# Writing the zeros of a block-inverse scratch during layer 0 instead of at the start of layer 1, in a two-layer S5 + HGRN2 | RWKV-7 decoder step

## The chip, the cores and the metric

One core of a Trainium2 chip runs the kernel. The metric is device time of one execution, in microseconds (us). The engines named below are PE (TensorE, matmuls), DVE (VectorE), ACT (ScalarE), POOL (GpSimd) and SP (SyncE), whose queue issues every DMA of this kernel.

## The reference

One inference step of a decoder trunk with two layers, model width 1024, in float32, for a prompt of 1024 tokens and 8 decode sequences of 4 tokens. Every product that matters is a dense float32 matrix product, or a recurrence over tokens:

```python
# layer 0 (even)
proj = xn @ w['even_w_in'][j]
u, z_a, q, f, i, z_b = jnp.split(proj, EVEN_SPLITS, axis=-1)
...                                  # S5 scan on u, HGRN2 on q, f, i
out = jnp.concatenate([out_a, out_b], axis=-1) @ w['even_w_out'][j]
h = h + out
# layer 1 (odd): token shift, then r, k, v, z and three low-rank products
xr, xw, xk, xv, xa, xg = (xn + xx * mix[m] for m in range(6))
r = xr @ wp[0]
...
s = (s * w_t[:, :, None, :]
     - jnp.einsum('bhvk,bhk->bhv', s, kk_t)[..., None] * (kk_t * a_t)[:, :, None, :]
     + v_t[..., None] * k_t[:, :, None, :])
```

The kernel computes the RWKV-7 recurrence in chunks. In each chunk the delta rule needs the inverse of a triangular matrix, which is taken in diagonal blocks of 32x32 and then combined; the 64x64 matrix that holds the diagonal blocks' inverses is zero beside them. These zeros are what the change is about.

## The kernel before

**Dense products.** Float32 is done as three fp32r matmuls: an operand is split into a high part (ACT copy, line 70) and the remainder (DVE subtract, line 72), so `xh,wh`, `xl,wh` and `xh,wl` appear as three matmuls. `dense2` (line 800; its matmuls are recorded at line 805) accumulates a whole product in a PSUM bank `dps`, of which there are two (line 798), and hands the bank to a function that empties it. Weights come as 256 KB loads into `ws`, and are split into `wh` and `wl`.

**DMAs.** `dma` (lines 51 and 52) issues everything on SP's queue, in program order as the scheduler leaves it. Staging tiles of tag "ev" (`evt`, line 1033, three buffers of 128x544) hold what goes from PSUM to DRAM.

**Layer 0** (`layer0`, line 1871). `proj_in` makes the input projection of one output tile after another and writes tiles to DRAM (`pr<-ev`); `s5_part` is the S5 branch, mostly on DVE; `hgrn_head` loads a head's tiles back (`hf<-pr`, `hq`, `hi`, `hz`) and begins with three activations on ACT (lines 567 to 569) and a scan on DVE. `run` (line 1860) takes turns between such generators by given rates, and thereby sets the order in which the program is written.

**Between the layers.** `proj_out` multiplies by `even_w_out` and adds the bank into the residual tile `res` on DVE (line 757), after `res<-xT` has loaded it; the sum is stored (`h<-res`).

**Layer 1.** `l1_constants` (line 889) loads and transposes the token-shift state (matmuls `t<-ident,ZB`), and then writes the zeros: a staging tile `sX` is cleared on POOL (line 902), and eight DMAs of 128x1024 (512 KB) write it to the four DRAM tiles `x_d` (`xd<-sX`, lines 903 to 905), 4.19 MB in all. `mixed` (line 929) makes the six mixed inputs `mm` on DVE, which are split into `xh`, `xl`. `rwkv_inverse` works out the diagonal blocks' inverses with 31 steps on DVE, in the same tile `sX` (cleared on POOL at line 1399), and writes only the blocks into `x_d`; later the chain of a batch loads whole matrices from there (`DT`). That chain also loads `ZR`, `BK` and `DA`.

**What sets the order.** The program is written by these generators, and a list scheduler with a timing model of its own then orders each engine's instructions. Each engine runs its stream in that order. An instruction that waits holds up all that follow it on its engine.

Of the kernel before, what the change touches and what calls it, by code (L numbers as in the profile page):

```python
# [36 lines left out]
class Builder:  # L37
# [837 lines left out]
    def l1_vectors(self):  # L875
# [8 lines left out]
        self.omix = K("omix", 6 * KT)  # L884
        self.nc.vector.tensor_scalar(out=self.omix, in0=self.mix, scalar1=-1.0, scalar2=1.0, op0=ALU.mult, op1=ALU.add)

    def l1_constants(self, kp):
        nc, V = self.nc, self.nc.vector
        K = lambda name, *sh: kp.tile([128, *sh], F32, name=name)
        sl = self.stage("ZB", 2, KT, 128)[:, 0]  # L890
        self.dma(sl[:8].rearrange("p k f -> p (k f)"), self.I["state_shift"][0])
        ps = self.PS(KT, NB)
        for k in range(KT):
            nc.tensor.transpose(ps[:, k], sl[:8, k], self.ident[:8, :8])
        self.evac(self.sh, ps, KT * NB)

        self.rs1 = K("rs1", 544)
        V.memset(self.rs1, 1.0)
        V.memset(self.rs1[:, 0:512].rearrange("p (n c) -> p n c", c=64)[:, :, 0:1], 0.0)
        V.memset(self.rs1[:, 512:544].rearrange("p (b t) -> p b t", t=NS)[:, :, 0:1], 0.0)  # L900
        zero = self.stage("sX", 32, 32)
        nc.gpsimd.memset(zero, 0.0)
        for d in self.x_d[0] + self.x_d[1]:
            for c in range(0, 8, 4):
                self.dma(d[:, c:c + 4].rearrange("r c p t -> r (c p t)"), zero[:].rearrange("r s t -> r (s t)"))

    def pair(self, n):
        self.pairs += 1
# [962 lines left out]
    def layer0(self, st):  # L1871
        tc = self.tc
        P = lambda name, st, **kw: st.enter_context(tc.tile_pool(name=name, bufs=1, reuse_waits="tile", **kw))
        self.pq = P("l0ps", st, space=PSUM)
        self.keep, hk, hp = P("l0k", st), P("hgk", st), P("hg", st)
        self.rbc = [self.keep.tile([128, 544], F32, name=f"rbc{i}") for i in range(2)]
        self.done, self.xn = set(), []
        order = [b + h for h in range(4) for b in (12, 8, 16, 20)] + list(range(4, 8))
        with ExitStack() as s5:
            kp = P("s5k", s5)  # L1880
            with ExitStack() as t:
                tp, xp = P("s5t", t), P("x0", t)
                self.sm = xp
                x1 = [self.normed(1, k, x) for k, x in enumerate(self.load_x(xp, 1, self.keep))]
                for m, _ in enumerate(self.proj_in(1, x1, range(4))):
                    if m == 1:
                        self.l1_vectors()
                    if m == 0:
                        x0 = self.load_x(xp, 0, self.keep)
                self.s5_params(kp, tp)  # L1890
                x0 = [self.normed(0, k, x) for k, x in enumerate(x0)]
                for _ in self.proj_in(0, x0, range(4)):
                    pass
            self.hgrn_constants(hk)
            sp = P("s5", s5)

            def dense():
                yield from self.proj_in(0, x0, order)
                x1 = self.reload_x(1)
                yield from self.proj_in(1, x1, order)  # L1900

            def s5s():
                for m in range(4):
                    for e in range(2):
                        yield from self.s5_part(sp, m, e)
                self.s5_finish(sp)

            def heads():
                for hf in range(2):
                    for h in range(4):  # L1910
                        while not all((k + h, hf) in self.done for k in (8, 12, 16, 20)):
                            yield
                        yield from self.hgrn_head(hp, hf, h)

            hgrn = heads()
            self.run((dense(), 1), (s5s(), self.rate0[0]), back=(hgrn, self.rate0[1]))
        ready = lambda hf: all(("o", hf, h) in self.done for h in range(4))
        self.heads, self.glus = ([], []), ([], [])
        with ExitStack() as t:
            gp = P("glu", t)  # L1920

            def rest():
                glu = self.glu(0, gp, gp)
                while not ready(0):
                    yield
                next(glu)
                self.heads_out(0, gp)
                yield from glu
                yield from self.proj_out(0)

            self.run((rest(), 1), (hgrn, self.rate0[2]))
# [82 lines left out]
```

## Time and profile before

| what | us |
|---|---|
| median of 3 runs | 1889.67 (1886.45, 1889.67, 1898.71) |
| the profiled execution | 1892.82 |
| its span on the engines | 1891.1 |
| PE busy | 1706.0 |
| DVE busy | 1297.9 |
| ACT busy | 977.1 |
| POOL busy | 140.7 |

The span runs from the first to the last instruction that the profile shows; 1.72 us of the profiled execution lie around it. A busy time is the sum over the instructions of an engine. The mean granted TensorE clock was 0.911 of full speed. The DMA engines moved 163 GB/s on the mean. Times within the trace are in us from the start of the span.

### The profile page before, as it was taken

The numbers are of one execution on the slowest core, as the hardware profiler recorded it, in microseconds if no ns is written. First come the engines' busy times: TensorE is split into PE (matmuls) and PEld (weight loads), VectorE is DVE, ScalarE is ACT, GpSimd is POOL, SyncE is SP. The second block draws the span as 40 slices with busy tenths as digits, with TensorE's granted clock in tenths as the row PEclk, the third lists the DMA queues.
The fourth block names the chain that finished last, engine by engine and source line by source line (L and its number), as shares of the span: only waits on it lengthen the run. The fifth ranks groups of instructions, "written<-read, shape, count | busy, mean of one in ns | idle before, by whom it ended". The sixth has DMA issues, their size and how long they took to land. (4 is left out here: it accounts for less than half of the span.)

```text
span 1891.1 us, 39586 instructions
## 1 busy us (share of the span) xinstructions
PE 1706.0 (90%) x15060; PEld 1419.1 (75%) x15060; DVE 1297.9 (69%) x3010; ACT 977.1 (52%) x1886; POOL 140.7 (7%) x257
## 2 busy tenths in 40 slices
PE   4999989999997698997399999998899999999867
PEld 3877868988876576775377778887798887788756
DVE  5797798875678624789598734868968566565554
ACT  5445555555645334643356766645555435434454
POOL 1210011000004200011021000000000000000000
PEclk9899999888999797998599889989898998999799
DMA  8555554444562556699758234589794666453453
GB/s 205 173 157 141 136 149 130 138 131 123 172 186 84 173 184 200 185 255 262 194 141 203 81 125 161 146 226 243 206 220 120 178 159 166 126 157 104 118 157 106
DMA packets 555010, 308.39 MB, mean 163 GB/s; under 512 B 284883, under 2 KB 489043, under 8 KB 554820
## 3 DMA queue, kind: packets, MB, share of 16 engines
q1 hardware_dynamic: 554820, 305.86, 59.1%
q8 instruction: 119, 1.95, 0.4%
q14 instruction: 71, 0.58, 0.1%
HBM read 199.76 MB, written 104.81 MB: 161 GB/s over the span
## 5 line engine op out<-in xcount | busy, mean ns | idle before, releaser
L805 PE MATMUL dps<-xh,wh 128*128 128x272 f32 (+3 forms) x1696 | 581.2, 349 | 55.3 <-ACT xh L70 22.3
L805 PE MATMUL dps<-xl,wh 128*128 128x272 f32 (+3 forms) x1696 | 582.6, 346 | 18.7 <-DVE xl L72 18.1
L805 PE MATMUL dps<-xh,wl 128*128 128x272 f32 (+3 forms) x1696 | 575.3, 342 | 4.8 <-DVE wl L72 4.7
L805 PEld LDWEIGHTS dps<-xh,wh 128*128 128x128 f32 x1696 | 330.9, 198 | 108.2 <-ACT xh L70 27.0
L805 PEld LDWEIGHTS dps<-xl,wh 128*128 128x128 f32 x1696 | 334.5, 198 | 60.9 <-DVE xl L72 28.1
L805 PEld LDWEIGHTS dps<-xh,wl 128*128 128x128 f32 x1696 | 335.0, 198 | 37.7 <-DVE wl L72 8.4
L70 ACT ACTIVATE wh<-ws 128x512 fp32r<-128x512 f32 (+1 forms) x336 | 195.9, 619 | 289.9 <-PE dps L805 198.8
L72 DVE TENSOR_TENSOR wl<-ws,wh 128x512 fp32r<-128x512 f32 (+1 forms) x336 | 224.1, 685 | 97.6 <-ACT wh L70 96.7
L1514 PE MATMUL m<-ZR,BK 64*128 64x128 f32 x512 | 62.8, 296 | 21.4 <-DMA ZR<-zr 20.6
L1514 PEld LDWEIGHTS m<-ZR,BK 64*128 64x128 f32 x512 | 54.0, 196 | 28.7 <-issue 14.3
L70 ACT ACTIVATE xh<-mm 128x256 fp32r<-128x256 f32 (+1 forms) x112 | 52.8, 481 | 37.5 <-DVE mm L929 19.7
L72 DVE TENSOR_TENSOR xl<-mm,xh 128x256 fp32r<-128x256 f32 (+1 forms) x112 | 55.6, 507 | 5.6 <-ACT xh L70 2.6
L805 PE MATMUL dps<-gh,wh 128*128 128x272 f32 (+1 forms) x176 | 55.8, 317 | 2.1 <-ACT ev L1106 1.1
L805 PE MATMUL dps<-gl,wh 128*128 128x272 f32 (+1 forms) x176 | 54.8, 312 | 1.4 <-DVE gl L72 1.4
L805 PE MATMUL dps<-gh,wl 128*128 128x272 f32 (+1 forms) x176 | 54.5, 310 | 0.1
L1411 DVE TENSOR_TENSOR sT<-sX,sN 128x31 f32<-128x31 f32 (+15 forms) x124 | 42.1, 339 | 11.9 <-DMA sN<-nd 10.2
L66 DVE COPY ev<-dps 128x272 f32<-128x272 f32 (+1 forms) x43 | 22.5, 526 | 40.2 <-PE dps L805 35.0
L64 ACT ACTIVATE ev<-dps 128x272 f32<-128x272 f32 (+1 forms) x65 | 29.3, 450 | 37.5 <-PE dps L805 37.1
L1571 PE MATMUL m<-ZM,DT 64*64 64x128 f32 x512 | 41.1, 291 | 2.4 <-DVE MR L1517 2.4
L1417 DVE TENSOR_TENSOR sX<-sX,sT 128x31 f32<-128x31 f32 (+15 forms) x124 | 42.0, 339 | 1.7
L863 POOL COPY edge<-h 128x1 f32<-128x1 f32 x8 | 27.1, 3392 | 182.6 <-DVE h L850 182.5
L805 PEld LDWEIGHTS dps<-gh,wh 128*128 128x128 f32 x176 | 35.1, 199 | 6.3 <-ACT ev L1106 1.6
(644 smaller groups left out, 3365.1 us busy)
## 6 DMA issues: line engine op xcount, KB each, us to landing
ws<-in_rw_w_rkvz SPq DMA_DIRECT2D x128, 256.0 KB, 4.2
ws<-in_even_w_in SPq DMA_DIRECT2D x96, 256.0 KB, 3.7
ws<-in_rw_w_o SPq DMA_DIRECT2D x48, 256.0 KB, 3.1
ws<-in_even_w_out SPq DMA_DIRECT2D x32, 256.0 KB, 3.8
BK<-bk SPq DMA_DIRECT2D x32, 256.0 KB, 4.4
ZR<-zr SPq DMA_DIRECT2D x32, 256.0 KB, 2.7
pr<-ev SPq DMA_DIRECT2D x20, 272.0 KB, 2.0
pr<-ev SPq DMA_DIRECT2D x20, 256.0 KB, 3.9
```

The lines of the kernel that those rows point to most:

```text
L64: return self.nc.scalar.activation(out, in_, AF.Copy)
L66: return self.nc.vector.tensor_copy(out, in_)
L70: self.nc.scalar.activation(hi, x, AF.Copy)
L72: e.tensor_tensor(out=lo, in0=x, in1=hi.bitcast(F32), op=ALU.subtract)
L805: mm = lambda c0, n, i, u, k, v: self.nc.tensor.matmul(ps[c0], u[:, k, :], v[:, c0:c0 + n], start=i == 0, stop=i == len(terms) - 1)
L863: G.tensor_copy(self.edge[:, k:k + 1], x[:, 512:513])
L1411: E.tensor_tensor(out=w, in0=X[:, s0:s0 + m, j:j + 1].broadcast_to([128, m, n]), in1=N[:, j, j + 1:32].unsqueeze(1).broadcast_to([128, m, ...
L1417: E.tensor_tensor(out=X[:, s0:s0 + m, j + 1:32], in0=X[:, s0:s0 + m, j + 1:32], in1=w, op=ALU.subtract)
L1514: nc.tensor.matmul(f2(pm[h][:, q]), f2(BK[hr, q]), f2(ZR[hr, q]), start=True, stop=True)
L1571: nc.tensor.matmul(pd[hr, q], DT[hr, q], ZM[hr, q], start=True, stop=True)
```

## The change

The zeros are written by a new generator, `clear_inverses`, which takes turns with the dense products and the S5 branch of layer 0 at a rate of 0.5. It clears 512 columns of one "ev" tile on POOL and issues 16 DMAs of 128x512 (256 KB), one at each turn. `l1_constants` loses the cleared tile and its eight DMAs. The bytes are the same.

```diff
--- before.py
+++ after.py
@@ -884,6 +884,15 @@
         self.omix = K("omix", 6 * KT)
         self.nc.vector.tensor_scalar(out=self.omix, in0=self.mix, scalar1=-1.0, scalar2=1.0, op0=ALU.mult, op1=ALU.add)
 
+    def clear_inverses(self):
+
+        zero = self.evt("zero")
+        self.nc.gpsimd.memset(zero[:, 0:512], 0.0)
+        for d in self.x_d[0] + self.x_d[1]:
+            for c in range(0, 8, 2):
+                self.dma(d[:, c:c + 2].rearrange("r c p t -> r (c p t)"), zero[:, 0:512])
+                yield
+
     def l1_constants(self, kp):
         nc, V = self.nc, self.nc.vector
         K = lambda name, *sh: kp.tile([128, *sh], F32, name=name)
@@ -898,11 +907,6 @@
         V.memset(self.rs1, 1.0)
         V.memset(self.rs1[:, 0:512].rearrange("p (n c) -> p n c", c=64)[:, :, 0:1], 0.0)
         V.memset(self.rs1[:, 512:544].rearrange("p (b t) -> p b t", t=NS)[:, :, 0:1], 0.0)
-        zero = self.stage("sX", 32, 32)
-        nc.gpsimd.memset(zero, 0.0)
-        for d in self.x_d[0] + self.x_d[1]:
-            for c in range(0, 8, 4):
-                self.dma(d[:, c:c + 4].rearrange("r c p t -> r (c p t)"), zero[:].rearrange("r s t -> r (s t)"))
 
     def pair(self, n):
         self.pairs += 1
@@ -1913,7 +1917,7 @@
                         yield from self.hgrn_head(hp, hf, h)
 
             hgrn = heads()
-            self.run((dense(), 1), (s5s(), self.rate0[0]), back=(hgrn, self.rate0[1]))
+            self.run((dense(), 1), (s5s(), self.rate0[0]), (self.clear_inverses(), 0.5), back=(hgrn, self.rate0[1]))
         ready = lambda hf: all(("o", hf, h) in self.done for h in range(4))
         self.heads, self.glus = ([], []), ([], [])
         with ExitStack() as t:
```

The scheduler's order changes with it. SP's queue in layer 0, where the dense products' weights (`ws`) are loaded and the first HGRN2 head's tiles (`pr_73` is its input `f`) are stored and loaded back; before, from the load of `ws` behind `u_88<-us`:

```order
L52 DMA ws<-in_even_w_in 128x4x128
L52 DMA pr_73<-ev 128x512
L52 DMA ws<-in_even_w_in 128x4x128
L52 DMA hf<-pr_73 128x512
L52 DMA pr_69<-ev 128x512
L52 DMA ws<-in_even_w_in 128x4x128 x2
L52 DMA hq<-pr_69 128x512
L52 DMA pr_77<-ev 128x512
L52 DMA ws<-in_even_w_in 128x4x128 x2
L52 DMA hi<-pr_77 128x512
```

and in the changed kernel, where the 16 writes `xd<-zero` stand from behind `u_88<-us` to ahead of `hq`:

```order
L52 DMA xd_121<-zero 128x512 x2
L52 DMA ws<-in_even_w_in 128x4x128
L52 DMA pr_73<-ev 128x512
L52 DMA ws<-in_even_w_in 128x4x128
L52 DMA xd_121<-zero 128x512 x2
L52 DMA xd_122<-zero 128x512 x2
L52 DMA hf<-pr_73 128x512
L52 DMA xd_122<-zero 128x512 x2
L52 DMA xd_123<-zero 128x512
L52 DMA pr_69<-ev 128x512
L52 DMA ws<-in_even_w_in 128x4x128
L52 DMA xd_123<-zero 128x512
```

Six of the 256 KB writes now stand ahead of `hf<-pr_73`, and the other ten between it and `hq`.

DVE in layer 0, where the first head's subtract (line 570) and scan (line 572) stand among the S5 branch's steps (lines 358 to 363) and the splits `wl`, as a piece of the difference:

```order
-L570 SCALAR_TENSOR_TENSOR hl<-hf,hl 128x512
 L361 TENSOR_SCALAR t_974<-t_974 128x256
 L359 TENSOR_TENSOR t_975<-ji 128x256
+L362 TENSOR_TENSOR jr<-jr,t_974 128x32x8
+L363 TENSOR_TENSOR ji<-ji,t_974 128x32x8
+L358 TENSOR_TENSOR t_974<-jr 128x256
+L72 TENSOR_TENSOR wl<-ws,wh 128x512
+L360 TENSOR_TENSOR t_974<-t_974,t_975 128x256
+L72 TENSOR_TENSOR wl<-ws,wh 128x512
+L361 TENSOR_SCALAR t_974<-t_974 128x256
+L570 SCALAR_TENSOR_TENSOR hl<-hf,hl 128x512
```

The two weight splits `wl` moved from behind the head's scan to ahead of the head's first DVE instruction.

DVE at the start of layer 1, where `res` is the first residual add of `proj_out` that follows the token-shift transposes, `mm` and `xl` are the mixed inputs and their low parts, and `blkm` and `hsel` are constants; before:

```order
L72 TENSOR_TENSOR wl<-ws,wh 128x512
L1219 CAST blkm<-e_6752 128x128
L72 TENSOR_TENSOR xl<-mm,xh 128x512 x2
L1254 COPY e_6800<-t 2x128 x4
L929 SCALAR_TENSOR_TENSOR mm<-df_6660,mix,h_6118 128x512
L929 SCALAR_TENSOR_TENSOR mm<-df_6666,mix,h_6157 128x512
L1255 CAST hsel<-e_6800 2x128 x4
L72 TENSOR_TENSOR xl<-mm,xh 128x512 x2
L929 SCALAR_TENSOR_TENSOR mm<-df_6672,mix,h_6196 128x512
L929 SCALAR_TENSOR_TENSOR mm<-df_6678,mix,h_6235 128x512
L72 TENSOR_TENSOR xl<-mm,xh 128x512 x2
L929 SCALAR_TENSOR_TENSOR mm<-df_6636,mix,h_5962 128x512
```

It goes on with one more `mm`, and then `L757 TENSOR_TENSOR res<-res,dps 128x272 x2`. In the changed kernel:

```order
L72 TENSOR_TENSOR wl<-ws,wh 128x512
L933 SCALAR_TENSOR_TENSOR mm<-df_6672,mix,h_6097 128x512
L72 TENSOR_TENSOR wl<-ws,wh 128x512
L757 TENSOR_TENSOR res<-res,dps 128x272 x2
L1223 CAST blkm<-e_6770 128x128
L72 TENSOR_TENSOR xl<-mm,xh 128x512 x2
L1258 COPY e_6818<-t 2x128 x4
L933 SCALAR_TENSOR_TENSOR mm<-df_6678,mix,h_6136 128x512
L933 SCALAR_TENSOR_TENSOR mm<-df_6684,mix,h_6175 128x512
L1259 CAST hsel<-e_6818 2x128 x4
L72 TENSOR_TENSOR xl<-mm,xh 128x512 x2
L933 SCALAR_TENSOR_TENSOR mm<-df_6690,mix,h_6214 128x512
```

The two adds `res` moved ahead of six splits `xl`, six mixed inputs `mm` and the constants, and the order of those is unchanged.

PE there, from the token-shift transposes `t<-ident,ZB` on, where the 512-column matmuls are the first product of layer 1 and those of 272 columns the next tile of `proj_out`; before:

```order
L894 MATMUL t<-ident,ZB 128x8 x8
L805 MATMUL dps<-xh,wh 128x512
L805 MATMUL dps<-xl,wh 128x512
L805 MATMUL dps<-xh,wl 128x512
L805 MATMUL dps<-xh,wh 128x512
L805 MATMUL dps<-xl,wh 128x512
L805 MATMUL dps<-xh,wl 128x512
L805 MATMUL dps<-xh,wh 128x512
L805 MATMUL dps<-xl,wh 128x512
L805 MATMUL dps<-xh,wl 128x512
L805 MATMUL dps<-xh,wh 128x512
```

It goes on with the rest of 24 matmuls of 512 columns, and then 48 of 272 columns. In the changed kernel:

```order
L903 MATMUL t<-ident,ZB 128x8 x8
L805 MATMUL dps<-xh,wh 128x512
L805 MATMUL dps<-xl,wh 128x512
L805 MATMUL dps<-xh,wl 128x512
L805 MATMUL dps<-xh,wh 128x512
L805 MATMUL dps<-xl,wh 128x512
L805 MATMUL dps<-xh,wl 128x512
L805 MATMUL dps<-xh,wh 128x512
L805 MATMUL dps<-gh,wh 128x272
L805 MATMUL dps<-gl,wh 128x272
L805 MATMUL dps<-gh,wl 128x272
```

The matmuls of 272 columns moved in between those of 512: behind the seven of 512 stand 14 of 272, then 5 of 512, 3 of 272, 1 of 512, 7 of 272, 11 of 512 and the last 24 of 272.

On SP's queue the load `res<-xT_57` stood behind the zeros (`ws<-in_rw_w_rkvz`, six `xd<-sX`, two `w2s`, two `xd<-sX`, `ws<-in_even_w_out`, `res<-xT_57`). In the changed kernel it stands right behind `ws<-in_rw_w_rkvz`.

## Rows read from the trace of the kernel before

**Rows 1.** The page: busy time, share of the span and instructions of each engine.

```profile
PE 1706.0 (90%) x15060; PEld 1419.1 (75%) x15060; DVE 1297.9 (69%) x3010; ACT 977.1 (52%) x1886; POOL 140.7 (7%) x257
```

**Rows 2.** Waits of PE: line, releaser, us in total, times, longest us.

```profile
PE m L1514 <- DMA ZR<-zr: 20.6, 2, 10.9
...
PE dps L805 <- DVE res L757: 17.5, 2, 15.3
```

**Rows 3.** PE's timeline, layer 1's start: start, us, then [idle before <-releaser].

```profile
627.87 0.66 PE L894 MATMUL t<-ident,ZB 8*128 8x8 f32 x8
643.87 0.77 PE L805 MATMUL dps<-xh,wh 128*128 128x512 f32 x1 [15.34 <-DVE res L757]
644.43 0.63 PE L805 MATMUL dps<-xl,wh 128*128 128x512 f32 x1
644.86 0.63 PE L805 MATMUL dps<-xh,wl 128*128 128x512 f32 x1
...
651.28 0.29 PE L805 MATMUL dps<-gh,wh 128*128 128x272 f32 x1
651.40 0.28 PE L805 MATMUL dps<-gl,wh 128*128 128x272 f32 x1
```

**Rows 4.** DVE's timeline there.

```profile
632.54 0.69 DVE L72 TENSOR_TENSOR wl<-ws,wh 128x512 fp32r<-128x512 f32 x1
...
640.69 1.35 DVE L72 TENSOR_TENSOR xl<-mm,xh 128x512 fp32r<-128x512 f32 x2
...
643.29 0.78 DVE L757 TENSOR_TENSOR res<-res,dps 128x272 f32<-128x272 f32 x2
```

**Rows 5.** SP's timeline there (its DMA issues).

```profile
625.75 0.43 SPq L52 DMA_DIRECT2D ws<-in_rw_w_rkvz  x1
626.28 5.65 SPq L52 DMA_DIRECT2D xd<-sX  x6
...
634.50 1.15 SPq L52 DMA_DIRECT2D xd<-sX  x2
...
636.50 1.28 SPq L52 DMA_DIRECT2D res<-xT  x1
```

**Rows 6.** Tile res, 600 to 720: time from issue to landing.

```profile
DMA to landing us min/median/max: 2.8/2.9/4.6
```

**Rows 7.** SP's timeline, layer 0.

```profile
108.52 0.52 SPq L52 DMA_DIRECT2D u<-us  x1
...
112.51 0.37 SPq L52 DMA_DIRECT2D ws<-in_even_w_in  x1
115.33 0.34 SPq L52 DMA_DIRECT2D hf<-pr  x1
```

**Rows 8.** ACT's timeline, layer 0.

```profile
118.19 0.64 ACT L567 ACTIVATE hl<-hf 128x512 f32<-128x512 f32 x1 [3.92 <-DMA hf<-pr]
...
122.71 1.13 ACT L70 ACTIVATE wh<-ws 128x512 fp32r<-128x512 f32 x2
```

**Rows 9.** Windows: PE, PEld, DVE, ACT, POOL busy (instructions), clock, DMA share, GB/s.

```profile
108.00:116.00 8.00, 8.00 (x36) 6.54 (x35) 8.00 (x52) 3.04 (x4) 0.00 (x0) 1.00 0.59 164
628.00:632.00 4.00, 0.53 (x8) 0.43 (x8) 3.82 (x13) 1.94 (x4) 0.00 (x0) 0.84 1.04 419
880.00:900.00 20.00, 9.81 (x81) 4.71 (x81) 17.67 (x42) 10.29 (x15) 6.45 (x12) 0.59 1.01 272
```

**Rows 10.** Tile ws, 108 to 130: time from issue to landing.

```profile
DMA to landing us min/median/max: 3.1/3.6/4.1
```

**Rows 11.** PE's timeline, layer 0.

```profile
124.38 0.50 PE L805 MATMUL dps<-xh,wh 128*128 128x512 f32 x1 [1.58 <-ACT ev L64]
...
127.19 0.80 PE L805 MATMUL dps<-xh,wl 128*128 128x512 f32 x1 [2.08 <-DVE wl L72]
```

**Rows 12.** PE's timeline, the chain of the first batches.

```profile
903.80 3.06 PE L1514 MATMUL m<-ZR,BK 64*128 64x128 f32 x16 [9.71 <-DMA ZR<-zr]
...
908.27 1.08 PE L1381 MATMUL t<-ZB 64*32 64x32 f32 x64
```

## The prediction

> **What bounds the kernel now.** I read the page's busy times first. PE is busy for 90% of the span, DVE for 69% [rows 1]. So over most of its length the kernel is a stream of matmuls, and a change of this kind can only win or lose in the places where PE stands still. The second view was the list of PE's waits. Two of its entries lie where this change works or just behind: 17.5 us for the residual add on DVE (line 757), of which 15.3 us in one piece, and 20.6 us for the load `ZR` [rows 2].
>
> The third view was PE's timeline around the long piece. PE ends the eight small transposes that begin at 627.87 and starts its next matmul at 643.87, after 15.34 us in which it waited for `res` on DVE [rows 3]. The two PSUM banks `dps` are full of an output-projection tile, and nothing else can go into them before DVE has added them into `res`. DVE's timeline tells why this comes late: the two adds stand in DVE's order behind a row of splits and mixed inputs. The split `wl` starts at 632.54, the last two `xl` end at 640.69 + 1.35 = 642.04, and the adds start at 643.29, with no idle time noted before any of these [rows 4]. In the same stretch SP issues the zeros, and `res<-xT` is issued at 636.50 behind them, where the weight load ahead of them went out at 625.75 [rows 5].
>
> **Layer 1's start, what is removed.** The eight writes of zeros go, and SP's 5.65 + 1.15 = 6.8 us of issuing them [rows 5]. The load of `res` then stands right behind the weight load, so it is issued at 625.75 + 0.43 = 626.2 and, with the usual 2.9 us and at most 4.6 us from issue to landing [rows 6], is there by 631. The adds stand behind the `wl` of 632.54, so they can start at 632.54 + 0.69 = 633.2 in place of 643.29, which is 10.1 us earlier. What is late next is PE's own work together with the `xl` splits. PE has 24 matmuls of 512 columns (643.87 to 651.28, 7.4 us with a slow start) and 48 of 272 columns, 0.12 us apart (5.8 us) [rows 3]. In the new order the two kinds alternate, so that PE can work on the second while DVE still makes the `xl` for the first. The last `xl` comes at 642.04 plus the 0.78 us of the adds, 642.8 [rows 4]. By then PE can have done the matmuls that don't need it, and the end of this piece moves from 651.28 + 5.8 = 657.1 to 633.8 + 13.2 = 647.0, a gain of 10.1 us. That is one bound. For the other I let the last 11 of the 512-column matmuls and 24 of the 272-column ones all wait for 642.8, at half the clock. Half the clock is the spacing of 644.43 and 644.86, 0.43 us, and twice 0.12 us for the short ones [rows 3]: 11 x 0.43 + 24 x 0.24 = 10.5 us, end 653.3, gain 3.8 us. I take 9.5, near the upper end, since the alternating order leaves PE enough to do before 642.8 (13 x 0.43 + 24 x 0.12 = 8.5 us of work for 9.0 us of time).
>
> **Layer 0, what is added.** 16 writes of 256 KB, 4.19 MB, go into SP's queue between `u<-us` at 108.52 and the load `hq`, six of them ahead of the load `hf`, which is issued at 115.33 [rows 7]. SP's issuing costs nothing by itself: SP has empty time between its issues there, such as 2.5 us ahead of 115.33, for 0.3 to 0.5 us an issue [rows 7]. What counts is the transfer. The window from 108 to 116 carries 164 GB/s. The highest rate that the trace shows, just when the zeros of before are written, is 419 GB/s; a stretch full of 256 KB loads reaches 272 GB/s, at a full DMA share too [rows 9]. In the 6.8 us from 108.52 to 115.33 the spare rate moves 1.73 MB at the one and 0.73 MB at the other, against six writes of 1.57 MB. So `hf` lands between 0 and (1.57 - 0.73) MB / 272 GB/s = 3.1 us late. ACT waits for it with nothing in hand (idle for 3.92 us until 118.19 [rows 8]), and its order is unchanged there, so the delay goes through ACT to the weight splits behind.
>
> For all 4.19 MB the same sum until 122.71 leaves 0.57 MB, or 1.4 us, at 419 GB/s, and 2.66 MB, or 9.8 us, at 272. A weight load has slack: issued at 112.51 [rows 7], landed after 3.6 us [rows 10], split at 122.71 [rows 8], 6.6 us spare. The excess is 0 to 3.2 us. With a restart of PE at half the clock (12 matmuls of 512 columns, 0.43 us [rows 3] in place of 0.12 x 512/272 = 0.23 us: 2.4 us) the worst is 3.1 + 3.2 + 2.4 = 8.7 us. Below nothing, the new order of DVE puts the `wl` splits ahead of the head's scan, and PE's two gaps there, 1.58 and 2.08 us [rows 11], may close: -3.7 us. I take +2, nearer to the 419 row because its transfers are the same writes, with two thirds of the 3.1 us for `hf`.
>
> The Trainium skill speaks against the smaller pieces. In "DMA: Bandwidth & Descriptors", section "Bandwidth", it asks for transfers of 1 MiB and gives 341 GB/s for 1 MB and 138 GB/s for 64 KB. [...]
>
> **The rest.** POOL clears one tile in either kernel, on an engine that is busy for 7% of the span [rows 1]: nothing. `zero` holds one of three "ev" tiles while the writes last; a store of `pr` that needs it would wait in the same stretch, which is inside the bound of 8.7 us. The scheduler's order moves almost everywhere by a few places. A single place that goes well or badly is worth about one of PE's larger waits, 9.7 us [rows 12], so I bound it by 10 us on either side and take nothing.
>
> **Sum.** 1892.82 - 9.5 + 2 = 1885.3 for an execution like the profiled one. That one lies 3.15 us above the median of 1889.67, so I predict 1882.2, rounded 1882. The bounds of the two priced terms give -13.8 to +4.9, or 1876 to 1895: this is the forecast's own range.
>
> **Rivals.**
> - *The gain is given back later, no change.* Around 880 to 900 the DMA engines are full (share 1.01) and PE is busy for less than half of the time [rows 9]; PE waits for `ZR` 20.6 us in all [rows 2]. If the loads there, and not PE, set the time, PE that comes 9.5 us earlier waits 9.5 us longer. What remains is the 2 us of layer 0: 1891.7. Against it: these loads and what fills them start earlier too when the stages ahead do, since the same queue issues everything.
> - *Slower: the zeros block layer 0.* `hf` is 3.1 us late, the last ten writes keep `hq` back by 9.8 us, ACT waits for both in its order, and PE runs out of split weights and restarts at half the clock (2.4 us): 15.3 us lost. The gap at layer 1's start gives 3.8. Then 1889.67 + 11.5 = 1901.2. It decides from the point where PE's lost time between 108 and 140 is over 9.5 us. For it: ACT's idle time before `hf`. Against: 6.6 us of slack in the weight loads, and a rate of 419 GB/s for such writes.
> The same skill page, section "Two DMAs through the same engine are not ordered", says that descriptors of one queue start in order on an engine; by that `hf` can't overtake the zeros. No row of before shows it.
> - *Faster by more: the first batches close a gap as well.* In the new order 32 of the small transposes `t<-ZB` (64 in the row at 908.27) stand ahead of the first `m<-ZR,BK`, where before they follow PE's wait of 9.71 us [rows 12]. If with them and the earlier start that wait closes: 1882.2 - 9.7 = 1872.5. Against it: 1.08 us of transposes fill little of it, and the load itself would have to come earlier.
>
> **Chances.** The forecast 0.59, no change 0.20, slower 0.09, faster by more 0.12. One per cent (18.9 us) is about what a measurement of this kernel can tell from no change: faster means 1870.8 or less, slower 1908.6 or more. The forecast's own range lies within 1%, and so does the rival without a change. The faster rival lies just inside, and I give half of it and a share of the unpriced order, 0.12, to faster; half of the slower one, 0.05, to slower. The range for 8 in 10 reaches from 1868, a little below the faster rival, to 1898, between the forecast's worst and the slower rival.
>
> **What would show it.** Right: PE's wait for `res` at layer 1's start shrinks from 15.34 to 5 or 6 us; the DMA share near 628 to 636 falls; `res<-xT` is issued near 626; in layer 0 `hf` lands by about 120 and PE's gaps between 120 and 130 stay within 6 us. The rest of the stages then keep their length and only start earlier. Wrong: the adds start late though `res` is there; PE's wait for `ZR` grows by what was won; `hq` or a split `wl` releases PE after a wait of several us near 120 to 140; or a wait of PE elsewhere, which this text does not name, grows or goes by 5 us or more.

## The result, and the profile of the changed kernel

The changed kernel takes 1907.74 us (median of 14 runs, 1901.03 to 1923.73), the kernel before 1896.8 us (14 runs on the same footing, 1886.19 to 1906.96). The ratio is 1.0071, 95% interval 1.005 to 1.0093: slower by 0.7%, outside the range of 1868 to 1898 us and on the other side of no change. The median of 1889.67 us that the forecast started from was that of three runs; the 14 lie 7 us higher, which explains part of the distance to 1882 but not the sign.

The profiled execution of the changed kernel took 1901.03 us, 8.2 us more than the one before. Its page, span and busy times first, as in [rows 1]:

```profile
span 1899.3 us, 39597 instructions
...
PE 1724.5 (91%) x15060; PEld 1433.6 (75%) x15060; DVE 1297.3 (68%) x3010; ACT 973.7 (51%) x1883; POOL 141.4 (7%) x257
```

PE's busy time grew from 1706.0 to 1724.5 us, by 18.5 us. Its idle time, span minus busy, fell from 1891.1 - 1706.0 = 185.1 to 1899.3 - 1724.5 = 174.8 us, by 10.3 us. So PE waited less, as was forecast, and yet took longer for the same 15060 matmuls: they ran at a lower clock. The granted clock of the profiled execution was 0.899, before 0.911. Each of these is one execution, and the clock also varies between executions of one order: x1 below, which has the order of the kernel before, has PE busy for 1731.8 us at 0.897 in its profile, more than the changed kernel:

```profile
PE 1731.8 (91%) x15060; PEld 1441.4 (75%) x15060; DVE 1298.8 (68%) x3010; ACT 977.6 (51%) x1886; POOL 145.7 (8%) x257
```

So the 18.5 us can't all be laid to the order. What can is shown further down: the times of all runs, their mean clock, and the stretches that agree over several profiles.

PE's waits in the changed kernel (line, releaser, us in total, times, longest), as in [rows 2]:

```profile
PE t L1385 <- DVE ZB L1340: 11.4, 2, 8.6
...
PE m L1518 <- DMA ZR<-zr: 8.1, 2, 7.6
PE m L1529 <- DVE Q L1596: 6.9, 2, 5.4
PE dps L805 <- DVE res L757: 6.1, 2, 5.4
```

The wait for `res` went from 17.5 to 6.1 us and the wait for `ZR` from 20.6 to 8.1 us. Two waits on DVE are new or grown: 11.4 us for `ZB`, and 6.9 us for `Q`, which was 0.6 us. Most of the first is no loss of its own. In the new order the transposes `t<-ZB` stand ahead of the first `m<-ZR,BK`, so PE waits 8.63 us for `ZB` where it waited 9.71 us for `ZR` [rows 12], and the wait for `DA` behind it is longer; the changed kernel, and then the kernel before:

```profile
894.75 1.08 PE L1385 MATMUL t<-ZB 64*32 64x32 f32 x64 [8.63 <-DVE ZB L1340]
...
914.56 0.70 PE L1552 MATMUL m<-DA,MZ 32*32 32x32 f32 x16 [11.43 <-DMA DA<-xnd]
```

```profile
919.61 0.81 PE L1548 MATMUL m<-DA,MZ 32*32 32x32 f32 x16 [8.62 <-DMA DA<-xnd]
```

Layer 1's start, the three rows that answer to [rows 3 to 5]: PE, DVE and SP of the changed kernel.

```profile
642.35 0.77 PE L805 MATMUL dps<-xh,wh 128*128 128x512 f32 x1 [5.36 <-DVE res L757]
```

```profile
641.77 0.78 DVE L757 TENSOR_TENSOR res<-res,dps 128x272 f32<-128x272 f32 x2
```

```profile
634.42 0.42 SPq L52 DMA_DIRECT2D ws<-in_rw_w_rkvz  x1
634.89 0.50 SPq L52 DMA_DIRECT2D res<-xT  x1
```

The load of `res` stands right behind the weight load (0.47 us, before 10.75 us behind it), the adds follow the second `wl`, and PE waits 5.36 us in place of 15.34. These are the steps as forecast.

Layer 0 of the changed kernel, SP and then ACT and PE, as in [rows 7, 8, 11]:

```profile
107.39 1.24 SPq L52 DMA_DIRECT2D xd<-zero  x2
...
111.28 2.61 SPq L52 DMA_DIRECT2D xd<-zero  x4
114.69 0.32 SPq L52 DMA_DIRECT2D hf<-pr  x1
115.06 1.46 SPq L52 DMA_DIRECT2D xd<-zero  x3
...
120.25 3.81 SPq L52 DMA_DIRECT2D xd<-zero  x6
```

```profile
119.07 0.63 ACT L567 ACTIVATE hl<-hf 128x512 f32<-128x512 f32 x1 [7.00 <-DMA hf<-pr]
```

```profile
125.26 0.80 PE L805 MATMUL dps<-xh,wh 128*128 128x512 f32 x1 [4.12 <-ACT ev L64]
```

`hf` is issued at 114.69 and starts ACT's activation at 119.07, 4.4 us later, where it took 2.9 us before. The 16 writes drive the DMA engines to their full share; the windows (PE, PEld, DVE, ACT, POOL busy, clock, DMA share, GB/s), as in [rows 9]:

```profile
108.00:116.00 8.00, 7.66 (x33) 5.63 (x32) 8.00 (x43) 3.04 (x4) 0.00 (x0) 1.00 1.02 312
116.00:124.00 8.00, 5.14 (x22) 3.86 (x21) 5.28 (x14) 4.87 (x7) 0.00 (x0) 0.95 1.05 358
```

PE's idle time there is one wait of 4.12 us, against 1.58 + 2.08 = 3.66 us before. In this execution PE waits 0.5 us more at this place.

Then one of the places where time went. In the stage of the batches PE works at half the clock while it is busy all the time. The windows of the changed kernel:

```profile
1030.00:1050.00 20.00, 18.62 (x259) 14.88 (x258) 16.52 (x42) 18.07 (x43) 0.00 (x0) 0.87 0.36 112
1050.00:1070.00 20.00, 20.00 (x125) 15.62 (x124) 14.78 (x40) 13.20 (x37) 0.00 (x0) 0.50 0.20 53
1070.00:1090.00 20.00, 20.00 (x127) 16.79 (x127) 6.37 (x15) 5.86 (x12) 0.00 (x0) 0.78 0.23 73
```

and of the kernel before, in which the same work runs about 8 us later:

```profile
1050.00:1070.00 20.00, 18.17 (x174) 14.06 (x174) 16.14 (x41) 15.72 (x39) 0.00 (x0) 0.66 0.24 69
1070.00:1090.00 20.00, 20.00 (x221) 17.58 (x216) 12.01 (x31) 10.96 (x27) 0.00 (x0) 1.00 0.28 85
```

From 1050 to 1090 PE of the changed kernel is busy for 40.00 of 40 us and gets through 252 matmuls; before, it gets through 395 in those 40 us, with 1.8 us idle (the two mixes of short and long ones are not the same). The trace's record of the granted clock has one stretch at half the clock of 34.1 us there (from 1044.8), where before it has one of 13.7 us (from 1054.0). No list of waits shows this, since nothing waits. The rows of PE around the fall:

```profile
1041.41 0.68 PE L1541 MATMUL m<-ident,ZR 64*64 64x64 f32 x16
1042.54 0.87 PE L1545 MATMUL m<-L,MZ 64*64 64x64 f32 x6 [0.45 <-ACT L L1576]
1043.91 0.39 PE L805 MATMUL dps<-xl,wh 128*128 128x272 f32 x1 [0.50 <-DVE xl L72]
...
1046.66 0.64 PE L1552 MATMUL m<-DA,MZ 32*32 32x32 f32 x16
```

and of the kernel before, where the clock falls at the same work:

```profile
1050.76 0.87 PE L1541 MATMUL m<-L,MZ 64*64 64x64 f32 x6 [0.93 <-DVE L L66]
...
1053.47 0.44 PE L1548 MATMUL m<-DA,MZ 32*32 32x32 f32 x16 [0.90 <-DVE ZM L66]
```

So the fall itself is in both kernels, with longer waits ahead of it in the old one. What differs is how long the half clock lasts behind it.

### The profile page after: what moved, and what is told of

Read it like the earlier page. It is cut to its first block, busy times and chain, and to the rows that moved or that the text cites. A ratio compares the mean times of both kernels' runs of the same rounds, so it can differ in the third digit from the quotient of the medians.

```text
span 1899.3 us, 39597 instructions
## 1 busy us (share of the span) xinstructions
PE 1724.5 (91%) x15060; PEld 1433.6 (75%) x15060; DVE 1297.3 (68%) x3010; ACT 973.7 (51%) x1883; POOL 141.4 (7%) x257
## 4 chain that ended last, share of the span: by engine, by line
PE 58%; DVE 17%; DMA 13%; ACT 6%; issue 3%; SPq 2%; POOL 0%; DVEq 0%; ACTq 0%; POOLq 0%
PE dps L805 33%; PE m L1518 2%; SPq L52 2%; DVE wl L72 2%; DVE xl L72 2%; PE xh L640 2%; DMA ws<-in_rw_w_o 1%; PE m L1575 1%; DVE sX L1421 1%; DMA ws<-in_rw_w_rkvz 1%; DVE sT L1415 1%; ACT wh L70 1%; PE m L1615 1%; DMA er<-rd 1%; DMA o<-o 1%
## 5 line engine op out<-in xcount | busy, mean ns | idle before, releaser
L805 PE MATMUL dps<-xh,wh 128*128 128x272 f32 (+3 forms) x1696 | 585.6, 352 | 52.9 <-ACT xh L70 18.8
L805 PE MATMUL dps<-xl,wh 128*128 128x272 f32 (+3 forms) x1696 | 582.0, 345 | 16.5 <-DVE xl L72 13.3
L805 PE MATMUL dps<-xh,wl 128*128 128x272 f32 (+3 forms) x1696 | 577.5, 343 | 2.8 <-DVE wl L72 2.4
L805 PEld LDWEIGHTS dps<-xh,wh 128*128 128x128 f32 x1696 | 333.1, 199 | 107.9 <-ACT xh L70 29.3
L805 PEld LDWEIGHTS dps<-xl,wh 128*128 128x128 f32 x1696 | 336.4, 199 | 54.9 <-DVE xl L72 19.9
L805 PEld LDWEIGHTS dps<-xh,wl 128*128 128x128 f32 x1696 | 336.9, 199 | 40.0 <-issue 6.6
L1518 PE MATMUL m<-ZR,BK 64*128 64x128 f32 x512 | 67.6, 310 | 8.3 <-DMA ZR<-zr 8.1
L805 PE MATMUL dps<-gh,wh 128*128 128x272 f32 (+1 forms) x176 | 55.6, 316 | 3.4 <-ACT ev L1110 1.7
L805 PE MATMUL dps<-gl,wh 128*128 128x272 f32 (+1 forms) x176 | 54.7, 311 | 1.4 <-DVE gl L72 1.4
L805 PE MATMUL dps<-gh,wl 128*128 128x272 f32 (+1 forms) x176 | 54.4, 309 | 0.1
L805 PEld LDWEIGHTS dps<-gh,wh 128*128 128x128 f32 x176 | 35.3, 201 | 7.9 <-ACT ev L1110 2.0
```

The source lines that it names most:

```text
L805: mm = lambda c0, n, i, u, k, v: self.nc.tensor.matmul(ps[c0], u[:, k, :], v[:, c0:c0 + n], start=i == 0, stop=i == len(terms) - 1)
L1518: nc.tensor.matmul(f2(pm[h][:, q]), f2(BK[hr, q]), f2(ZR[hr, q]), start=True, stop=True)
```

## The experiments

**How the order was held.** The programs of both kernels hold the same instructions apart from the zeros: 10805 on PE, 3010 on DVE, 1763 on ACT, 254 on POOL, and on SP 1648 besides the 8 or 16 writes. So an experiment can take the program of one and the order of the other. A function was added that chains each engine's instructions in a given order (issue order alone, no semaphore), and a table `ORDER` of the positions:

```diff
+def pin(tc, rows):
+    traced = list(tc.nc.cur_bb.bb.instructions)
+    for row in rows:
+        at = 0
+        last = None
+        for step in row:
+            at += step
+            if last is not None:
+                tc.add_manual_dep(traced[at], last.name, mybir.DependencyInfo(
+                    mybir.DependencyClass.NoSync, mybir.DependencyReason.DATA), reason="pin")
+            last = traced[at]
...
         Builder(tc, I, O).build()
+        pin(tc, json.loads(zlib.decompress(base64.b85decode(ORDER))))
```

The function moves the lines of these kernels by 17: `L822` in their rows is `L805` above, and `L774` is `L757`. "Old order" is that of the kernel before, "new order" that of the changed kernel. A piece is a range of each engine's instructions that holds the same instructions in both orders. The theory ORDER says that the scheduler's new order of everything else costs the time; the rival WRITES says that the zeros' writes in layer 0 do.

**Whole orders crossed: x1 and x2.**

```diff
 x1: program of the changed kernel
-    ORDER: its own
+    ORDER: old, with the 16 writes of zeros behind the same neighbours on SP
 x2: program of the kernel before
-    ORDER: its own
+    ORDER: new, with the 8 writes of zeros behind the same neighbour on SP
```

> The changed program (16 writes of zeros in layer 0), with every other instruction of every engine held in the order of the kernel before; no zeros at layer 1's start. Theory ORDER (the writes cost under 2 us; the loss is in the order that the scheduler made of everything else): within 4 us of the kernel before, ratio 0.998 to 1.002; the residual adds still stand late on DVE, so PE's wait of about 15 us at layer 1's start stays. Rival WRITES (the zeros delay layer 0): at least 8 us slower than the kernel before, ratio 1.004 or more.

> The kernel before (8 writes of zeros at layer 1's start), with every other instruction held in the order of the changed kernel (one clearing of sX on POOL is moved behind four masks). ORDER: as slow as the changed kernel or up to 6 us slower, since the load of res may land behind the zeros: ratio 1.005 to 1.011. WRITES: as the kernel before or faster, ratio under 1.001.

x1: 1896.83 us, ratio 1.0008 (0.9979 to 1.0036). x2: 1908.88 us, ratio 1.0074 (1.0049 to 1.0099). The time follows the order, not the place of the zeros. WRITES falls: in x1 the writes stand in layer 0 and the time is that of before, within an interval of some 0.3% to either side. The price of the writes alone can be read there; PE's rows of x1 in layer 0 and at layer 1's start:

```profile
125.00 0.50 PE L822 MATMUL dps<-xh,wh 128*128 128x512 f32 x1 [3.97 <-ACT ev L81]
...
127.81 0.80 PE L822 MATMUL dps<-xh,wl 128*128 128x512 f32 x1 [2.08 <-DVE wl L89]
```

```profile
647.37 0.76 PE L822 MATMUL dps<-xh,wh 128*128 128x512 f32 x1 [15.00 <-DVE res L774]
```

3.97 + 2.08 = 6.05 us of waits in layer 0 against 3.66 before [rows 11]: 2.4 us. The 15 us wait at layer 1's start is still there (15.00), though no zeros are written near it. So taking the zeros away does not shorten this wait by itself: DVE's order held the adds.

**Only the start of layer 1: x4, x9, x12.**

```diff
 x4: program of the changed kernel
-    ORDER: its own
+    ORDER: old, with the pieces around the first residual add (66 of PE, 23 of DVE, 4 of SP) new
 x9: program of the kernel before
-    ORDER: its own
+    ORDER: old, with the same pieces of PE and DVE new, and on SP:
 L69 DMA ws<-in_rw_w_rkvz 128x4x128
+L69 DMA res<-xT_57 128x544
 L69 DMA xd_121<-sX 128x1024 x2
...
-L69 DMA res<-xT_57 128x544
 x12: x9 without the move of res on SP
```

> The changed program in the order of the kernel before, except for the pieces of DVE, PE and SP around layer 1's first residual add, which stand as in the changed kernel. ORDER: the 15 us wait shrinks to about 5 us and nothing else moves: 7 to 11 us faster than the kernel before, ratio 0.994 to 0.997. WRITES: the gain is eaten in layer 0, ratio 0.999 to 1.004.

> The kernel before with its zeros where they were, in its own order, but for the pieces of DVE, PE and SP around layer 1's first residual add as in the changed kernel, and the load of res ahead of the zeros. If the 15 us wait came from DVE's order alone: as x4_start_only, 7 to 11 us faster than the kernel before, ratio 0.994 to 0.997. If the zeros' transfers held it too: 0 to 5 us faster, ratio 0.998 to 1.001.

> x9_zeros_stay with SP as in the kernel before: the load of res stands behind the zeros, and the residual adds stand early on DVE. If the zeros hold the load (issued at about 636, landed at 639): DVE waits 5 to 6 us at the adds, PE's wait shrinks to 9 to 11 us in place of 5, and the kernel is 2 to 6 us slower than x9, ratio 0.996 to 0.999. If the load is not held: as x9, 0.993 to 0.996.

x4: 1888.88 us, ratio 0.9963 (0.9941 to 0.9985). x9: 1884.1 us, ratio 0.9948 (0.9916 to 0.9981). x12: 1898.33 us, ratio 1.0004 (0.998 to 1.0028), slower than was expected, and with a longer wait of PE than the 9 to 11 us expected. PE's wait is 4.93 us in x4, 5.40 us in x9 and 13.81 us in x12, in this sequence:

```profile
638.17 0.76 PE L822 MATMUL dps<-xh,wh 128*128 128x512 f32 x1 [4.93 <-DVE res L774]
```

```profile
635.79 0.77 PE L822 MATMUL dps<-xh,wh 128*128 128x512 f32 x1 [5.40 <-DVE res L774]
```

```profile
642.42 0.77 PE L822 MATMUL dps<-xh,wh 128*128 128x512 f32 x1 [13.81 <-DVE res L774]
```

Why x12 wins nothing stands in its SP and DVE rows:

```profile
626.59 5.68 SPq L69 DMA_DIRECT2D xd<-sX  x6
...
636.67 1.29 SPq L69 DMA_DIRECT2D res<-xT  x1
```

```profile
632.72 0.68 DVE L89 TENSOR_TENSOR wl<-ws,wh 128x512 fp32r<-128x512 f32 x1
641.83 0.78 DVE L774 TENSOR_TENSOR res<-res,dps 128x272 f32<-128x272 f32 x2 [8.43 <-DMA res<-xT]
```

With the adds early on DVE, DVE itself waits 8.43 us for the load of `res`, which is issued at 636.67 behind the zeros; the adds start 5.2 us after that. So the gap had two causes in a row: DVE's order, and behind it the place of `res` in SP's queue. Both have to go, and x9 shows that the zeros can stay where they were if `res` goes ahead of them; there it is issued 0.47 us behind the weight load:

```profile
627.71 0.42 SPq L69 DMA_DIRECT2D ws<-in_rw_w_rkvz  x1
628.18 0.50 SPq L69 DMA_DIRECT2D res<-xT  x1
628.78 5.58 SPq L69 DMA_DIRECT2D xd<-sX  x6
```

x4 and x9 beat both kernels. Their difference, 0.15%, is inside their intervals.

**Where the new order costs time: x5 to x8.**

```diff
 x5: x4, and from the output projection (about 551 us) on all engines
-    ORDER: old
+    ORDER: new
 x6: x5, and from about 1000 to 1290 us
-    ORDER: new
+    ORDER: old
 x7: x4, and from about 1000 to 1290 us
-    ORDER: old
+    ORDER: new
 x8: x4, and layer 0's branches (up to about 551 us)
-    ORDER: old
+    ORDER: new
```

> The changed program, in the order of the kernel before up to the end of layer 0's two branches and in that of the changed kernel from the output projection on. If the loss comes from layer 0's order alone: 5 to 12 us faster than the kernel before, ratio 0.994 to 0.998. If it comes from layer 1's order alone: 6 to 15 us slower, ratio 1.003 to 1.008. If from both, in between.

> The changed program; order of the kernel before in layer 0, of the changed kernel from the output projection on, except for the piece of about 1000 to 1290 us (the stage of the first batches), which stands as in the kernel before. If the loss sits in that piece (PE there at half the clock while busy, and two waits): 12 to 22 us faster than x5_new_from_projection, ratio 0.990 to 0.996. If it is spread over the new order: 2 to 6 us faster than x5, ratio 0.999 to 1.002.

> x4_start_only, with the piece of about 1000 to 1290 us in the order of the changed kernel. If the loss sits there: 12 to 20 us slower than x4, ratio 1.002 to 1.007 to the kernel before. If it is spread: within 5 us of x4, ratio 0.994 to 0.999.

> x4_start_only, with layer 0's two branches in the order of the changed kernel. By the profiles (PE's work of 300 to 500 us takes 162 to 165 us there, against 154 to 157 in the old order): 6 to 10 us slower than x4, ratio 0.999 to 1.003 to the kernel before. If layer 0's order is worth nothing: ratio 0.994 to 0.998.

x5: 1901.8 us, ratio 1.0027 (1.0001 to 1.0054). x6: 1895.64 us, ratio 1.0012 (0.9975 to 1.0049). x7: 1916.56 us, ratio 1.0135 (1.0076 to 1.0194, five runs). x8: 1896.54 us, ratio 1.001 (0.9986 to 1.0035). Against x4's 0.9963, layer 0's new order costs 0.5% (x8) and everything from the projection on 0.6% (x5); together these are the 1.1% between x4 and the changed kernel. The piece of the batches' stage alone costs 1.7% (x7), more than the 1.002 to 1.007 expected and more than x5, which contains it. x7's profile does not show where: it is that of its fastest run, 1898.87 us. x6 is a miss for the theory that all the loss sits in that piece: with the piece taken back the kernel is only 0.15% below x5, inside the intervals. So the pieces of layer 1 do not add up.

To see where the time goes, the traces were cut at matmuls that stand at the same place in both orders, by the program's count of PE's instructions (10805, where the profile lists 15060). Each column is one profiled execution. Each cell is the time of the stretch, of it at half the clock by the clock record, and of it with PE idle, in us:

```
PE's instructions     before            x1                x4                changed           x2                x5                x6
1450-2318 (layer 0)   156.5 30.7  4.4   156.6 30.7  4.4   157.1 30.7  4.8   165.4 44.4  8.6   162.6 41.0  8.3   154.1 23.8  5.0   152.8 20.5  5.3
2500-2828 (start)      95.7 26.5 27.5    95.2 26.1 27.1    85.1 16.9 16.4    85.6 17.1 16.8    90.3 19.7 23.1    85.9 14.5 17.2    85.9 20.2 16.8
3525-4190             161.4 61.4 39.8   160.0 58.0 38.3   160.6 61.4 37.8   154.2 54.6 34.4   155.5 58.0 33.7   155.0 51.2 34.1   157.2 51.2 35.0
4190-4601              79.5  0.0  3.1    82.8  8.5  2.8    80.0  0.0  3.9    81.7  0.0  3.8    82.7  0.0  4.7    80.3  0.0  3.0    85.3  9.2  3.8
4601-5090              70.8 13.7  2.0    71.4 15.4  2.0    69.4 10.2  2.0    80.5 34.1  1.6    81.0 34.1  1.8    80.9 34.1  1.8    70.9 14.7  2.0
5090-5500              66.5 13.7  1.7    74.0 30.7  2.1    74.1 30.7  2.5    71.4 27.3  0.9    68.8 20.5  0.9    66.5 17.1  0.6    74.1 30.7  2.3
5941-6484              67.7 17.1  3.8    64.6 13.7  2.6    65.6 13.7  3.4    72.6 20.5  8.2    72.7 20.5  8.2    74.4 20.5 10.7    75.8 27.3  9.8
```

Before and x1 have the old order in every row, the changed kernel and x2 the new one. x4 has the old one but for the start; x5 and x6 have it in layer 0, and x6 also from 4601 on. The start wins 10 us (5 in x2, where `res` is issued behind six of the zeros' writes) and 3525 to 4190 some 6 us; layer 0 loses some 8 (x8: 168.4 us), 4601 to 5090 some 10, and 5941 to 6484 some 7 us. In 4601 to 5090 the idle time does not change: all of the loss is time at half the clock. x7 has 80.9 us there too, and x8, x9 and x12, with the old order, 69.4 to 70.2.

One order also varies between profiles: layer 0 takes 152.8 us (x6) to 161.3 us (x14) in the old one. And part of the 10 us comes back right behind: 5090 to 5500 takes 74.0 to 74.1 us in six profiles of the old order (x1, x4, x6, x8, x9, x12), 66.5 and 67.1 in those of before and x11, and 66.5 to 71.4 in the new. Over 4601 to 5500 the new order takes 147.4 to 151.9 us (changed, x2, x5, x7), the old one 143.5 to 145.4 in these six, and 137.3 and 138.7 in before and x11. Against the six, the loss there is nearer to 5 us than to 10.

In x6, 4601 to 5090 is back at 70.9 us. The stretches around it that are longer than in x5 are mostly what the old order takes elsewhere: 74.1 us for 5090 to 5500, and for 4190 to 4601 85.3 us with 9.2 at half the clock, where x1 has 82.8 with 8.5. Only 5941 to 6484, which ends at the piece's seam at 1290 us, is out of line: 75.8 us, where the old order takes 61.1 to 67.7 in the other profiles.

**The batches' stage taken apart: x10, x13, x14, x11.**

```diff
 x10: x4, and from about 1070 to 1106 us
-    ORDER: old
+    ORDER: new
 x13: x4, and from about 1000 to 1070 us
-    ORDER: old
+    ORDER: new
 x14: x4, and from about 1070 to 1290 us
-    ORDER: old
+    ORDER: new
 x11: x9, and from about 794 to 1005 us, and from about 1380 us on
-    ORDER: old
+    ORDER: new
```

> x4_start_only, with one piece of 36 us (about 1070 to 1106 us in the kernel before: 261 matmuls of PE and the instructions of ACT, DVE and SP beside them) in the order of the changed kernel. If this piece's order keeps PE at half the clock: the stretch of PE's work that takes 69 to 71 us in the old order takes 80 us, with about 34 us of it at half the clock, and the kernel is 6 to 12 us slower than x4, ratio 0.999 to 1.003. If the half clock comes from what stands ahead of the piece: stretch and ratio (0.994 to 0.998) as x4.

> x4_start_only, with the piece of about 1000 to 1070 us of every engine in the order of the changed kernel; the narrow piece behind it, to 1106 us, stays in the old order. If what stands in this piece sends PE to half the clock: the stretch of PE's work of 69 to 71 us takes 76 to 81 us with 24 to 34 us of it at half the clock, and the kernel is 6 to 12 us slower than x4, ratio 1.000 to 1.004. If it takes both pieces together: stretch and ratio (0.994 to 0.998) as x4.

> x4_start_only, with the piece of about 1070 to 1290 us of every engine in the order of the changed kernel, the complement of x13 within x7. If the waits of 5.4 and 2.8 us of PE near 1260 to 1280 us of the changed kernel come from this piece's order: PE's work that takes 65 us there takes 72 us or more, and the kernel is 6 to 17 us slower than x4, ratio 1.000 to 1.006. If not: ratio 0.994 to 0.998.

> x9_zeros_stay, with two more pieces in the order of the changed kernel in which its profiles are shorter: about 794 to 1005 us, and from about 1380 us to the end. If the times of pieces add up: 6 to 11 us faster than x9, ratio 0.989 to 0.993 to the kernel before. If the seams between the pieces cost what they win: ratio 0.994 to 0.998.

x10: 1895.62 us, ratio 1.0011 (0.9989 to 1.0032). Its profile has 72.4 us for the stretch 4601 to 5090, 15.2 us of it at half the clock: the narrow piece does not bring the half clock back, while the ratio is 0.5% above x4's, outside what was expected for that case (0.994 to 0.998). What the 0.5% is, its profile does not show: that execution is 2.5 us shorter than x4's. x13: 1901.9 us, ratio 1.0043 (1.002 to 1.0066). x14: 1899.04 us, ratio 1.0034 (1.0009 to 1.0059). Against x4 these are 0.8% and 0.7%, together 1.5%, about the 1.7% of x7. The profiles show different things in the two halves. x13, windows from 1040 us, beside those of x4:

```profile
1040.00:1060.00 20.00, 18.81 (x262) 14.97 (x258) 16.49 (x43) 17.73 (x42) 0.00 (x0) 0.87 0.32 99
1060.00:1080.00 20.00, 20.00 (x140) 16.35 (x138) 13.54 (x36) 10.80 (x30) 0.00 (x0) 0.50 0.20 54
```

```profile
1040.00:1060.00 20.00, 18.01 (x196) 13.88 (x194) 18.00 (x45) 17.79 (x45) 0.00 (x0) 0.74 0.36 103
1060.00:1080.00 20.00, 20.00 (x223) 17.24 (x223) 12.51 (x34) 10.90 (x28) 0.00 (x0) 1.00 0.26 83
```

In x13 PE is busy for 20.00 of 20 us from 1060 to 1080 and has half the clock throughout, where x4 has the full one; x13's record has 27.3 us at half from 1055, x4's 10.2 us from 1048, and 4601 to 5090 takes 76.4 us in x13. A second cost of x13 is a wait of 5.32 us for a split on ACT:

```profile
1004.09 0.80 PE L1666 MATMUL t<-e,blk 128*128 128x512 f32 x1 [5.32 <-ACT e L87]
```

x14's profile takes 80.2 us for 5941 to 6484 (11.9 idle, 30.7 at half the clock), where x4's takes 65.6 (3.4 and 13.7). It has two waits of the changed kernel, for `Q` and the later one for `ZB` on DVE, nearly to the digit; x14 and then the changed kernel:

```profile
1261.77 0.69 PE L1546 MATMUL m<-ident,v 128*128 128x128 f32 x2 [5.34 <-DVE Q L1613]
...
1278.76 0.58 PE L1402 MATMUL t<-ZB 64*32 64x32 f32 x44 [2.93 <-DVE ZB L1357]
```

```profile
1261.88 0.69 PE L1529 MATMUL m<-ident,v 128*128 128x128 f32 x2 [5.36 <-DVE Q L1596]
...
1278.73 0.58 PE L1385 MATMUL t<-ZB 64*32 64x32 f32 x44 [2.82 <-DVE ZB L1340]
```

DVE's row of the changed kernel ahead of `Q` shows what it waits for:

```profile
1257.31 1.29 DVE L1331 TENSOR_TENSOR_SCAN e<-rs,es 128x544 f32<-128x544 f32 x1 [3.02 <-DMA es<-swd]
...
1261.41 0.41 DVE L1596 TENSOR_TENSOR Q<-ZR,m 128x256 f32<-128x256 f32 x1
```

A scan that waits 3.02 us for the load `es` stands ahead of `Q` on DVE, with other work between them, and `Q` is what PE waits for 5.36 us. No run moved the scan alone.

x11: 1893.82 us, ratio 0.9981 (0.9957 to 1.0005). The first piece is shorter in its profile, as in the changed kernel (3525 to 4190: 156.1 us in place of x9's 162.5), but the stretch with the seam at 1380 us, 6836 to 7497, is 93.9 us in place of 84.2, with 13.8 us idle in place of 3.5; all other profiles have 83.1 to 87.3. In this profile the seam costs more than the piece wins.

**The clock over all runs.** The mean granted clock of each kernel's runs goes with its time: before 0.906 to 0.908 (four groups of runs have 0.9060, 0.9063, 0.9064 and 0.9077), x1 0.906, x4 0.908, x9 0.908, x12 0.907, x10 0.906, x6 0.905, x8 and x13 0.904, the changed kernel 0.901, x2 0.898, x5 0.902, x7 0.900. x14 (0.906, ratio 1.0034) and x11 (0.909, ratio 0.9981) do not follow it. x11's profile has 5 us more idle time than x9's (173.5 against 168.2 us). For x14 no such difference shows: PE is idle for 175.4 us in its profile and for 177.2 in x4's.

## Why the prediction was wrong

- **The gain at layer 1's start: right.** Forecast 9.5 us, bounds 3.8 to 10.1. The stretch of PE's work there went from 95.7 to 85.6 us, and x4, which has only this gain and the writes, is 9.4 us below the median of before beside it. The order of the terms was right too: the adds early on DVE and `res` early in SP's queue. What the text did not see is that the move of the zeros was not needed for it (x9) and did not cause it (x1): the new order did.
- **The price of the writes in layer 0: right.** Forecast +2 us, bounds -3.7 to 8.7. x1 shows 2.4 us of waits more, the changed kernel 0.5. (What layer 0's new order costs later, 0.5% in x8, belongs to the next term.) The writes ran beside 164 GB/s of other traffic at 312 to 358 GB/s in all, between the two rates weighed (419 and 272), and `hf` started ACT 0.9 us later; whether it overtook any of the six writes issued ahead of it, no run shows. The Trainium skill ("DMA: Bandwidth & Descriptors", section "Bandwidth") gives 138 GB/s for loads of 64 KB and no figure for 256 KB; at 138 GB/s the 4.19 MB of zeros would take 30 us, an estimate. The trace does not bear that out for these 256 KB writes: all 16 were issued from 107.39 to 124.06 us, with 312 to 358 GB/s in all from 108 to 124.
- **The rest of the order: the step that failed.** The text said that "a single place that goes well or badly is worth about one of PE's larger waits", bounded it by 10 us on either side and took nothing, without a reason for that middle. From x4 to the changed kernel the order alone makes 1.0071 / 0.9963 = 1.0108, some 20 us. It is not one place but several of 5 to 10 us with both signs (table above), 0.5% in layer 0 (x8) and 0.6% behind it (x5). And the bound was read from PE's waits, where part of the cost doesn't show: in 4601 to 5090 the order adds 10 us with 2 us idle either way, all at half the clock. A rearranged order can change the clock that is granted to the same matmuls. The last sign that the text named for being wrong did come: waits elsewhere, for `ZB` and `Q`, went up by more than 5 us.
- **The rivals.** The slower one named layer 0's writes, at 15.3 us; they cost 0.5 to 2.4, so the kernel is slower for another reason. "The gain is given back later" was right as a form, not in its mechanism: in x4, which has the gain and the old order behind it, PE waits for `ZR` for 20.7 us, against 20.6 before, and keeps the gain. The faster rival happened in part and by another way: with the transposes ahead, the first wait for `ZR` closed, but the wait for `ZB` took its place (8.63 us). The stretch 3525 to 4190 is still 6 to 7 us shorter; that is the order and not the earlier start, for x4 has 160.6 us there. It was outweighed.
- **The range** was built from the two priced terms and one unpriced place. With both signs and some five such places, three of which lost time, the unpriced term needed more width. That it needed it more upwards than downwards is known only from the result.

What stays open: which instruction's place in the piece from 1000 to 1070 us keeps PE at half the clock. x13's one profile shows it with that piece (27.3 us at half the clock), and x10's does not with what follows alone. The order of PE alone over the whole piece was not tried. Why this stage's new order costs 1.7% in x7, but x5, which has it too, loses only 0.6%, stays open as well.

## What to carry to other kernels

Where a scheduler orders the instructions, a small edit is two changes: the one in the diff, and a new order everywhere; hold the old order and put only the edit into it (or only the piece of the order that wins) before crediting the edit with the time. Here the edit by itself was worth nothing that could be measured (x1), the new order of one place was worth -0.4 to -0.5%, and the rest of the new order +1.1%. Read PE's busy time and granted clock per stretch beside its waits: time lost at half the clock has no waiter. And read them in more than one profile of an order, since x1 and the kernel before, with one order, differ by 25.8 us of PE's busy time.

## What the runs showed of the hardware

In the stretch 4601 to 5090 TensorE stayed at half the clock, 1.2 GHz, for 34.1 us in each of the four profiles with the new order from 1000 to 1106 us (the changed kernel, x2, x5, x7), and for 10.2 to 15.4 us in the seven with the old order there (before, x1, x4, x6, x8, x9, x12). In the changed kernel the half clock ran from 1044.8 to 1079.0, and TensorE was busy for 40.00 of 40 us from 1050 to 1090. Ahead of the fall it did short matmuls (64x64), with waits of 0.45 and 0.50 us; the kernel before did the same with waits of 0.93 and 0.90 us, and was back at full clock after 13.7 us.

Runs of one kernel spread by 11 us in x8 and by 26 us in x6 (1887.15 to 1913.38), and the slower runs tend to have the lower granted clock: x1's fastest run took 1888.69 us at 0.909, its slowest 1913.03 us at 0.897.
